# Gate and up projection of the second token half by seven block products, with the down projection summed in DRAM

## The chip, the cores and the metric

One core of a Trainium2 chip runs the whole program. The metric is the device time of one execution in microseconds (us). The engines are PE (matrix multiply; PEld is its weight load), ACT and DVE (element-wise), POOL and SP (here they mostly issue transfers). SBUF is the on-chip memory and PSUM the small memory that PE writes and that ACT and DVE read. DRAM is reached by transfers ("DMAs") which 16 DMA engines carry out.

## The reference

The reference is one transformer-like block on 2048 tokens of 1024 features: a state-space branch, a convolution branch, a merge, and a gated feed-forward network ("FFN") with a final norm. What matters here is its last part.

```
def _swiglu(h, wg, wu, wd):
    return (jax.nn.silu(h @ wg) * (h @ wu)) @ wd
...
        x = x + g2 * _swiglu(_modulate(x, norm2_g[l], sh2, sc2), w_ffn_gate[l], w_ffn_up[l], w_ffn_down[l])
...
    return _rmsnorm(x, norm_f_g)
```

The hidden width FFN_HIDDEN is 2816, which is 22 column tiles of 128. `wg` and `wu` are 1024 by 2816 and `wd` is 2816 by 1024, all 32-bit floats.

## The kernel before, in words

Tokens are handled in two halves of 1024 (HALF). Features lie on the partitions and tokens along the free axis. The 32-bit product is made of three PE products: each operand is split into a rounded part "hi" and a remainder "lo", and `gemm` (L181) issues hi by hi, hi by lo and lo by hi for each 128 features, all into one PSUM sum. The names tell the parts: `h2h`/`h2l` are the two parts of the normalised input, `ah`/`al` those of the hidden activations, `hi`/`lo` those of a weight tile. `wload` loads 512 KB of weights into `raw`, ACT makes `hi` (L159) and DVE `lo` (L161); there are two buffers each of raw, hi and lo.

`ffn` goes through the 22 hidden tiles in chunks of 2, 4, 4, 4, 4 and 4. For each hidden tile it computes gate (48 matmuls of 512 tokens: 8 feature blocks, 3 products, 2 token blocks) and up (48 more); ACT applies silu to gate (L1168), DVE multiplies by up (L1175), and `split` makes ah (ACT, L193) and al (DVE, L194). After a chunk come its "downs": for each of 8 output tiles m, PE multiplies ah/al by the down weights and DVE adds the result, times the modulation, to an SBUF accumulator `acc[m]` (L1190), which had been loaded once with the residual from the DRAM array `d_x1`. In the last chunk the downs run for tokens 0 to 511 and then for 512 to 1023; ACT squares the second lot (L1193) and DVE sums the squares (L1195).

Work beside this runs as "background" generators (`bg`): at each k step of a matmul group `tick` gives them credit, and they emit some of their instructions there. `h2` normalises the input that way (L1141 to 1144), and `final` the finished first 512 tokens (transposes L1244, Square L1247, `newton` L140 to 146 for the reciprocal root, scaling L1249). `final_last` does the last 512 tokens by matmuls with a diagonal of gains (L1225, L1232, L1233). `gains` builds that diagonal ahead of the second half's FFN (transpose L1206).

PSUM has eight banks of 512 numbers per partition. `mm` hands out tiles of two banks (three of them), `ms` tiles of one bank (two). `t4` hands out one of four SBUF buffers of 128 by 1024 numbers. A buffer is given out again once its last reader is done. Within one engine instructions run in the order of its list, so what stands behind a waiting instruction waits too. A scheduler fixes these lists when the program is built; blocks marked `high_priority` are drawn ahead in them.

Of the kernel before, what the change touches and what calls it, by code (L numbers as in the profile page):

```python
# [1524 lines left out]
```

## Time and profile before

| | |
|---|---|
| median of 3 runs | 3040.83 us (3038.77 to 3044.93) |
| the profiled execution's own time | 3038.56 us |
| its span from first to last instruction | 3036.8 us |
| mean granted PE clock | 0.991 |
| PE busy | 2963.6 us, 98% of the span |
| DVE busy | 1990.7 us, 66% |
| ACT busy | 905.9 us, 30% |

All times of single instructions come from the profiled execution. PE's row of busy time is a union of overlapping matmuls; a granted clock of 1.00 is 2.4 GHz and 0.50 is 1.2 GHz. The FFN of the second half runs from about 2200 us to the end.

### The profile page before, as it was taken

What the parts mean: (1) busy time and instruction counts of PE and PEld (TensorE: products, weight loads), DVE (VectorE), ACT (ScalarE), POOL (GpSimd) and SP (SyncE); (2) the same over time, 40 slices, a digit from 0 to 9 for tenths busy, and PEclk for the clock granted to TensorE, in tenths of its full rate; (3) what the DMA queues carried; (4) which work ended last, traced back from release to release, by engine and by line L of the source; (5) the groups of instructions that cost most, each with busy time, mean ns of one, the idle gap of its engine ahead of it and who ended that gap; (6) DMA issues with size and microseconds to landing.
All of it is one profiled execution on the core that took longest, in us unless ns stands there. A gap on an engine that the chain in (4) does not pass through costs nothing.

```text
span 3036.8 us, 34166 instructions
## 1 busy us (share of the span) xinstructions
PE 2963.6 (98%) x13227; PEld 2403.5 (79%) x13227; DVE 1990.7 (66%) x2932; ACT 905.9 (30%) x1235; POOL 172.9 (6%) x313
## 2 busy tenths in 40 slices
PE   7999999999999999999999999999999999999999
PEld 3778787878878777778888888888887888888887
DVE  6489899997897576767787887756666232322225
ACT  4323344334443562233212112134233111111112
POOL 0111321100011000000000000000000000000000
PEclk8999999999999999999999999999999999999999
DMA  5344545534443468865222222223556111111112
GB/s 202 125 124 127 156 151 185 175 94 124 125 121 110 156 202 289 273 199 184 69 63 63 63 63 72 67 97 122 190 179 203 56 49 49 49 49 49 49 49 104
DMA packets 386754, 370.36 MB, mean 122 GB/s; under 512 B 31841, under 2 KB 334273, under 8 KB 386592
## 3 DMA queue, kind: packets, MB, share of 16 engines
q1 hardware_dynamic: 347168, 280.97, 29.8%
q0 software_dynamic: 25968, 82.46, 7.6%
q10 hardware_dynamic: 13456, 4.75, 0.7%
q8 instruction: 104, 1.70, 0.2%
q14 instruction: 58, 0.48, 0.0%
HBM read 280.42 MB, written 87.67 MB: 121 GB/s over the span
## 4 chain that ended last, share of the span: by engine, by line
issue 66%; PE 20%; DVE 5%; DMA 5%; POOL 2%; ACT 1%; ACTq 0%; POOLq 0%; DVEq 0%; SPq 0%
PE mm L181 17%; DVE acc L919 2%; DMA wm<-in_w_mod_dram 2%; PE ms L740 1%; DMA d_xt<-xts 1%; DVE lo L161 1%; DMA ma<-d_ma 1%; POOL d_x L1111 1%; PE ms L695 1%; DMA d_in<-st 0%; DMA Braw<-in_ssm_b_re_dram 0%; DMA dwr<-in_dw_kernel_dram 0%; PE ms L805 0%; PE ms L806 0%; DVE mr L345 0%
## 5 line engine op out<-in xcount | busy, mean ns | idle before, releaser
L159 ACT ACTIVATE hi<-raw 128x1024 fp32r<-128x1024 f32 (+1 forms) x280 | 293.1, 1047 | 1317.7 <-PE mm L181 1259.9
L919 DVE SCALAR_TENSOR_TENSOR acc<-cin,dwk,acc 128x1009 f32<-128x1009 f32 (+1 forms) x464 | 570.3, 1270 | 1.1 <-ACT acc L915 0.5
L181 PE MATMUL mm<-h2h,hi 128*128 128x512 f32 x1408 | 548.6, 390 | 0.0
L181 PE MATMUL mm<-h2l,hi 128*128 128x512 f32 x1408 | 547.9, 389 | 0.1
L181 PE MATMUL mm<-h2h,lo 128*128 128x512 f32 x1408 | 547.8, 389 | 0.0
L161 DVE TENSOR_TENSOR lo<-raw,hi 128x1024 fp32r<-128x1024 f32 (+1 forms) x280 | 337.0, 1204 | 267.2 <-ACT hi L159 266.1
L181 PE MATMUL mm<-hh,hi 128*128 128x512 f32 x1152 | 479.1, 416 | 0.5 <-ACT hh L445 0.5
L181 PE MATMUL mm<-hl,hi 128*128 128x512 f32 x1152 | 454.7, 395 | 0.0
L181 PE MATMUL mm<-hh,lo 128*128 128x512 f32 x1152 | 453.8, 394 | 0.0
L181 PEld LDWEIGHTS mm<-h2l,hi 128*128 128x128 f32 x1408 | 264.4, 188 | 55.6 <-DVE h2l L1144 0.7
L181 PEld LDWEIGHTS mm<-h2h,hi 128*128 128x128 f32 x1408 | 264.3, 188 | 55.5 <-issue 0.5
L181 PEld LDWEIGHTS mm<-h2h,lo 128*128 128x128 f32 x1408 | 264.3, 188 | 54.7 <-DVE lo L161 0.2
L181 PE MATMUL mm<-ah,hi 128*128 128x512 f32 x704 | 274.5, 391 | 0.0
L181 PE MATMUL mm<-al,hi 128*128 128x512 f32 x704 | 273.8, 390 | 0.0
L181 PE MATMUL mm<-ah,lo 128*128 128x512 f32 x704 | 273.5, 389 | 0.0
L181 PEld LDWEIGHTS mm<-hh,lo 128*128 128x128 f32 x1152 | 218.1, 189 | 47.0 <-issue 0.4
L181 PEld LDWEIGHTS mm<-hh,hi 128*128 128x128 f32 x1152 | 218.1, 189 | 46.6 <-issue 2.2
L181 PEld LDWEIGHTS mm<-hl,hi 128*128 128x128 f32 x1152 | 218.5, 190 | 44.5 <-issue 1.4
L1175 DVE TENSOR_TENSOR fg<-mm,fg 128x1024 f32<-128x1024 f32 (+1 forms) x48 | 54.5, 1134 | 271.9 <-PE mm L181 266.6
L1190 DVE SCALAR_TENSOR_TENSOR x<-mm,mod,x 128x1024 f32<-128x1024 f32 (+1 forms) x104 | 124.6, 1199 | 162.6 <-PE mm L181 162.3
L181 PEld LDWEIGHTS mm<-ah,hi 128*128 128x128 f32 x704 | 132.1, 188 | 31.1 <-ACT ah L193 4.0
L181 PEld LDWEIGHTS mm<-al,hi 128*128 128x128 f32 x704 | 132.2, 188 | 28.5 <-DVE al L194 1.2
(376 smaller groups left out, 3718.6 us busy)
## 6 DMA issues: line engine op xcount, KB each, us to landing
raw<-in_w_in_dram SPq DMA_DIRECT2D x72, 512.0 KB
wm<-in_w_mod_dram SPq DMA_DIRECT2D x48, 512.0 KB
raw<-in_w_ffn_gate_dram SPq DMA_DIRECT2D x48, 512.0 KB
raw<-in_w_ffn_up_dram SPq DMA_DIRECT2D x48, 512.0 KB
raw<-in_w_ffn_down_dram SPq DMA_DIRECT2D x44, 512.0 KB
d_g<-gsig POOLq DMA_DIRECT2D x32, 512.0 KB, 4.5
raw<-in_w_out_dram SPq DMA_DIRECT2D x32, 512.0 KB
d_vp<-vsig POOLq DMA_DIRECT2D x16, 512.0 KB, 3.7
```

What stands on the lines that cost most here:

```text
L159: nc.scalar.activation(hi, raw, AF.Copy)
L161: nc.vector.tensor_tensor(lo, raw, hi.bitcast(F32), op=OP.subtract)
L181: nc.tensor.matmul(ps[:, b * bw : (b + 1) * bw], wt[:, k, c0 : c0 + 128], mv[k][:, b * bw : (b + 1) * bw], start=(k == 0 and j == 0), stop ...
L695: nc.tensor.matmul(pz[:, d, :], BD[:, d, i, r, :], CR[d][r][:, i, d : d + 8].rearrange("p j c -> p (j c)"), start=(r == 0), stop=(r == 1))
L740: nc.tensor.matmul(ps.rearrange("p (i m) -> p m i", i=8), IN[:, d, i, :], rhs, start=True, stop=True)
L919: self.behind(nc.vector.scalar_tensor_tensor(t, x[:, i : i + W], K(i), t, op0=OP.mult, op1=OP.add), LAG)
L1111: nc.gpsimd.dma_start(self.d_x1[m, :, ts], xt)
L1175: nc.vector.tensor_tensor(g, pu[:, cs], g, op=OP.mult)
L1190: nc.vector.scalar_tensor_tensor(acc[m][:, cs], ps[:, cs], self.mod2[:, 24 + m : 25 + m], acc[m][:, cs], op0=OP.mult, op1=OP.add)
```

## The change

The change concerns the second token half only. For one hidden tile, gate and up together are a product of a 2 by 2 block matrix of weights (gate and up; features 0 to 511 and 512 to 1023: A11, A12, A21, A22) with a 2 by 2 block matrix of inputs (the same two feature blocks; tokens 0 to 511 and 512 to 1023: B11, B12, B21, B22). Before, that is eight block products of 12 matmuls each. After, it is seven, by sums of blocks: S1 = A21 + A22, S2 = S1 - A11, S3 = A11 - A21, S4 = A12 - S2 for the weights, and T1 = B12 - B11, T2 = B22 - T1, T3 = B22 - B12, T4 = B21 - T2 for the inputs. The T blocks are made once (`sums_first`, `sums_last`), in the background of the first chunk; the S blocks for each hidden tile (`group_weights`). One hidden tile is then a `group` of 84 matmuls in place of 96: A11 B11, S1 T1, S2 T2, A12 B21, S3 T3, S4 B22 and A22 T4. Partial sums stay in PSUM: b1 and b2 are the two banks of one `mm` tile, b3 is an `ms` tile. Some of them are copied to the SBUF tiles `fg` and `fu` on the way (`copy` on ACT) and added later (`add` on DVE).

The SBUF that held the accumulators now holds these operands. So the downs are no longer summed in SBUF: ACT scales each result into a `t4` tile `fd`, and POOL issues a DMA that adds it to `d_x1` in DRAM. All chunks have 2 hidden tiles (11 chunks; the first is computed as before, by eight products). For the last chunk the sums are loaded back and finished as before. `gains` moves from the start of the FFN to after it. Cut to its core:

```
+    def prod(self, ps, w, c0, x, start=True, stop=True, group=True):
+
+        nc = self.nc
+        (whi, wlo), (xhi, xlo) = w, x
+        n = len(xhi)
+        for k in range(n):
+            for j, (wt, mv) in enumerate(((whi, xhi), (whi, xlo), (wlo, xhi))):
+                nc.tensor.matmul(
+                    ps,
+                    wt[:, k, c0 : c0 + 128],
+                    mv[k],
+                    start=start and k == 0 and j == 0,
+                    stop=stop and k == n - 1 and j == 2,
+                    skip_group_check=not group,
+                )
+            self.tick()
+
...
+    def group_weights(self, vp, t):
+
+        nc = self.nc
+        TT = nc.vector.tensor_tensor
+        col = slice(t * 128, (t + 1) * 128)
+        gate, up = (self.A[n][0, :, col].rearrange("(k p) c -> p k c", p=128) for n in ("w_ffn_gate", "w_ffn_up"))
+        with self.tc.high_priority():
+            w4 = self.wp.tile([128, 8, 128], F32, tag="raw", name=self.nm("wu"))
+            nc.sync.dma_start(w4, up)
+            w1, w2, w3 = (vp.tile([128, HALF], F32, tag="acc", name=self.nm("ws"), bufs=3).rearrange("p (k c) -> p k c", c=128) for _ in range(3))
+            a, b = slice(0, 4), slice(4, 8)
+            nc.sync.dma_start(w1[:, a], gate[:, a])
+            nc.sync.dma_start(w2[:, b], gate[:, b])
+            TT(w1[:, b], w4[:, a], w4[:, b], op=OP.add)
+            TT(w2[:, a], w1[:, b], w1[:, a], op=OP.subtract)
+            p1 = self.parts(w1)
+            TT(w3[:, a], w1[:, a], w4[:, a], op=OP.subtract)
+            TT(w3[:, b], w2[:, b], w2[:, a], op=OP.subtract)
+            p2 = self.parts(w2)
+            p3 = self.parts(w3)
+            p4 = self.parts(w4[:, b], 512)
+        cut = lambda p, s: tuple(t[:, s] for t in p)
+        return {"A11": cut(p1, a), "S1": cut(p1, b), "S2": cut(p2, a), "A12": cut(p2, b), "S3": cut(p3, a), "S4": cut(p3, b), "A22": p4}
+
+    def group(self, vp, t, X, ah, al):
+
+        nc = self.nc
+        W = self.group_weights(vp, t)
+        ps, b3 = self.mm(), self.ms()
+        b1, b2 = ps[:, 0:512], ps[:, 512:1024]
+        g, u = self.t4(name="fg"), self.t4(name="fu")
+        L, R = slice(0, 512), slice(512, 1024)
+        copy = lambda o, i: nc.scalar.activation(o, i, AF.Copy)
+        add = lambda o, i: nc.vector.tensor_tensor(o, i, o, op=OP.add)
+        hp = self.tc.high_priority
+        self.prod(b1, W["A11"], 0, X["B11"], group=False)
+        with hp():
+            copy(g[:, L], b1)
+        self.prod(b2, W["S1"], 0, X["T1"], group=False)
+        with hp():
+            copy(u[:, R], b2)
+        self.prod(b1, W["S2"], 0, X["T2"], start=False, group=False)
+        with hp():
+            copy(g[:, R], b1)
+        self.prod(b3, W["A12"], 0, X["B21"])
+        with hp():
+            add(g[:, L], b3)
+            nc.scalar.activation(g[:, L], g[:, L], AF.Silu)
+        self.prod(b1, W["S3"], 0, X["T3"], start=False, group=False)
+        with hp():
+            add(u[:, R], b1)
+        self.prod(b2, W["S4"], 0, X["B22"], start=False, group=False)
+        with hp():
+            add(g[:, R], b2)
+            nc.scalar.activation(g[:, R], g[:, R], AF.Silu)
+            nc.vector.tensor_tensor(u[:, R], u[:, R], g[:, R], op=OP.mult)
+        self.prod(b1, W["A22"], 0, X["T4"], start=False, group=False)
+        with hp():
+            nc.vector.tensor_tensor(u[:, L], b1, g[:, L], op=OP.mult)
+            self.split(u, ah, al)
+        self.dve(12)
...
+        for c in range(11):
+            if c:
+                for t in range(2):
+                    self.group(vp, c * 2 + t, X, *a[t])
+                    yield "up"
+            if c == 10:
+                break
+            for m4 in range(2):
+                w = down(c, m4)
+                for m in range(4):
+                    ps = self.mm()
+                    for b in range(2):
+                        self.prod(ps[:, b * 512 : (b + 1) * 512], w, m * 128, halves[b])
+                    o = self.t4(name="fd")
+                    nc.scalar.activation(o, ps, AF.Copy, scale=self.mod2[:, 24 + m4 * 4 + m : 25 + m4 * 4 + m])
+                    nc.gpsimd.dma_start(self.d_x1[m4 * 4 + m, :, hs], o, accum_op=OP.add)
+                    yield "down"
+        acc = [self.slot("Q", F32, name="x1") for _ in range(8)]
+        rs.append(self.slot("P", F32, (128, 512), name="rsf"))
+        with self.tc.high_priority():
+            for m in range(8):
+                nc.gpsimd.dma_start(acc[m], self.d_x1[m, :, hs])
+        end.append(acc)
+        for b in range(2):
+            bs = slice(b * 512, (b + 1) * 512)
+            for m in range(8):
+                if m % 4 == 0:
+                    w = down(10, m // 4)
+                ps = self.mm()[:, bs]
+                self.prod(ps, w, (m % 4) * 128, halves[b])
+                nc.vector.scalar_tensor_tensor(acc[m][:, bs], ps, self.mod2[:, 24 + m : 25 + m], acc[m][:, bs], op0=OP.mult, op1=OP.add)
+                if b:
+                    sq = rs[0] if m == 0 else self.t4(shape=(128, 512), name="sq")
+                    nc.scalar.activation(sq, acc[m][:, bs], AF.Square)
+                    if m:
+                        nc.vector.tensor_tensor(rs[0], rs[0], sq, op=OP.add)
+                self.dve()
+                yield "down"
...
+        X, rs, end = {}, [], []
+        e = self.bg(self.h2s_first(1, r[2], X))
         take(self.out_proj(1, mg[1], vp, 512, 512, r))
         self.finish(e)
-        acc = []
-        dg = self.gains(vp)
-        rs = [vp.tile([128, HALF], F32, tag="acc", name="rsf", bufs=3)[:, 0:512]]
-        f1 = self.ffn(1, h2[1], "P", acc, 1, rs)
-        e = self.bg(self.h2(1, r[3], "Q", h2, 512, 512))
+        X["raw"] = [self.slot("P", F32, name="bf") for _ in range(4)]
+        for n in ("T2", "T3"):
+            X[n] = self.operand("P", n)
...
+        def sums():
+            yield from self.sums_first(X)
+            yield (W_SUM,)
+            yield from self.sums_last(X)
+
+        e = self.bg(sums())
+        take(f1, 2 + 8)
+        self.finish(e)
+        take(f1, 10 * 2 + 9 * 8 + 8)
+        acc = end[0]
+        dg = self.gains()
         e = self.bg(self.final(1, acc, 0, 4))
         take(f1)
         self.finish(e)
```

The lists of the engines show where the new instructions stand. The first place is ACT while gate and up are computed. Before, its list for a hidden tile and the start of the next reads as follows: `fg` from `mm` is the silu of gate, `ah` the first part of the activations, `hi` that of the next weights.

```order
L1168 ACTIVATE fg_19053<-mm_19004 128x1024 [waits PE_49]
L159 ACTIVATE hi_19174<-raw_19172 128x1024 [waits DMAHW2_49,DVE_49,PE_49]
L193 ACTIVATE ah_19110<-fg_19053 128x1024 [waits DVE_49]
L159 ACTIVATE hi_19234<-raw_19232 128x1024 [waits DMAHW3_49,PE_49,Activation_49]
L1168 ACTIVATE fg_19170<-mm_19121 128x1024 [waits PE_49]
```

After, one group on ACT. `fg` and `fu` from `mm` are the copies of partial sums (L1346), L1361 and L1368 the two silus, L1309 the first parts of S and A weights (`ws`, `wu`), and the last line the split.

```order
L1346 ACTIVATE fg_18356<-mm_18354 128x512 [waits DMASW2_49,PE_49,Activation_49]
L1309 ACTIVATE hi_18346<-ws_18331 128x1024 [waits DVE_49,PE_49]
L1346 ACTIVATE fu_18357<-mm_18354 128x512 [waits DMASW3_49,PE_49,Activation_49]
L1309 ACTIVATE hi_18350<-wu_18327 128x512 [waits DMAHW2_49,DVE_49,PE_49]
L1346 ACTIVATE fg_18356<-mm_18354 128x512 [waits PE_49]
L1361 ACTIVATE fg_18356<-fg_18356 128x512 [waits DVE_49]
L1309 ACTIVATE hi_18463<-ws_18456 128x1024 [waits DMAHW0_49,PE_49,Activation_49]
L1368 ACTIVATE fg_18356<-fg_18356 128x512 [waits DVE_49]
L1309 ACTIVATE hi_18469<-ws_18457 128x1024 [waits DMAHW1_49,PE_49,Activation_49]
L194 ACTIVATE ah_16974<-fu_18357 128x1024 [waits DVE_49]
```

Before, ACT reads PSUM once for each hidden tile (L1168). Now it reads it three times (L1346), a weight part stands between each two of these reads, and that part itself waits for PE, since it goes into a buffer from which PE has to be done.

The second place is PE. Before, its list at the step from gate to up of a hidden tile reads:

```order
L181 MATMUL mm_19644<-h2l_16657,hi_19640 128x512
L181 MATMUL mm_19644<-h2h_16649,lo_19642 128x512
L181 MATMUL mm_19704<-h2h_16642,hi_19700 128x512 [waits Activation_49]
L181 MATMUL mm_19704<-h2l_16650,hi_19700 128x512
L181 MATMUL mm_19704<-h2h_16642,lo_19702 128x512 [waits DVE_49]
```

In that list one product ends, and the next begins in another PSUM tile. After, a group's list from the end of S2 T2 over one matmul of A12 B21 (`ms`) to the start of S3 T3 reads:

```order
L1295 MATMUL mm_18354<-T2h_16967,lo_18344 128x512
L1295 MATMUL ms_18355<-B21h_16651,lo_18344 128x512
L1295 MATMUL mm_18354<-T3h_16970,hi_18346 128x512 [waits Activation_49]
L1295 MATMUL mm_18354<-T3l_16972,hi_18346 128x512
L1295 MATMUL mm_18354<-T3h_16970,lo_18348 128x512 [waits DVE_49]
```

S3 T3 goes into the PSUM tile of S2 T2. The step from S3 T3 to S4 B22, a few matmuls on, reads:

```order
L1295 MATMUL mm_18354<-T3h_16971,hi_18346 128x512
L1295 MATMUL mm_18354<-T3l_16973,hi_18346 128x512
L1295 MATMUL mm_18354<-T3h_16971,lo_18348 128x512
L1295 MATMUL mm_18354<-B22h_16654,hi_18346 128x512 [waits DVE_49]
L1295 MATMUL mm_18354<-B22l_16656,hi_18346 128x512
```

Before, the new gate or up product goes to another PSUM tile (`mm_19704` in place of `mm_19644`), and the waits are for weights. After, all products but A12 B21 go to the same tile `mm_18354`. The wait of S3 T3 is for the copy of `fg` out of that tile (the fifth ACT line above), the wait of S4 B22 for DVE's add of `fu` out of it, and S1 T1, S2 T2 and A22 T4 begin with a wait of the same kind. A group's 12 matmuls of A12 B21 stand in three lots: 4 between A11 B11 and S1 T1, 7 between S1 T1 and S2 T2, and 1 as shown.

On DVE the same group ends with this run: the `add` of `fg` from b3, the second part of A22's weights, the `add` of `fu` from b1, the `add` of `fg` from b2, work for the next group, and the two products.

```order
L1347 TENSOR_TENSOR fg_18356<-ms_18355,fg_18356 128x512 [waits DMASW6_49,DMASW2_49,PE_49]
L1311 TENSOR_TENSOR lo_18352<-wu_18327,hi_18350 128x512 [waits Activation_49]
L1347 TENSOR_TENSOR fu_18357<-mm_18354,fu_18357 128x512 [waits DMASW7_49,DMASW3_49,PE_49]
L1347 TENSOR_TENSOR fg_18356<-mm_18354,fg_18356 128x512 [waits PE_49,Activation_49]
L1311 TENSOR_TENSOR lo_18465<-ws_18456,hi_18463 128x1024 [waits Activation_49]
L1369 TENSOR_TENSOR fu_18357<-fu_18357,fg_18356 128x512 [waits Activation_49]
L1327 TENSOR_TENSOR ws_18723<-wu_18721 128x512 [waits DMAHW2_49,DVE_49]
L1372 TENSOR_TENSOR fu_18357<-mm_18354,fg_18356 128x512 [waits PE_49]
```

Before, DVE read PSUM once for each hidden tile here (L1175); now it does so four times (L1347 three times, L1372).

The third place is PE at the end of the program. Before, the transposes of `final` (`ident`) stand between the last downs:

```order
L181 MATMUL mm_21115<-ah_20744,hi_21094 128x512
L181 MATMUL mm_21115<-al_20745,hi_21094 128x512
L181 MATMUL mm_21115<-ah_20744,lo_21096 128x512
L1244 MATMUL mm_21132<-ident,x_2392_16976 128x128 [waits DVE_49,PE_49]
L1244 MATMUL mm_21132<-ident,x_2393_16977 128x128
```

So the list has 128x128 transposes among 128x512 matmuls. After, the last down and the first transposes read:

```order
L1295 MATMUL mm_21532<-ah_16976,hi_21495 128x512
L1295 MATMUL mm_21532<-al_16977,hi_21495 128x512
L1295 MATMUL mm_21532<-ah_16976,lo_21497 128x512
L1493 MATMUL mm_21545<-ident,x_3010_21339 128x128 [waits DMASW6_49,DVE_49]
L1493 MATMUL mm_21545<-ident,x_3011_21340 128x128 [waits DMASW7_49]
```

Three sets of eight transposes follow one another; behind the third the list goes on with the sums over the squares (`rsf`) and the products with the gains (`gfd`):

```order
L1493 MATMUL mm_21603<-ident,x_3016_21345 128x128
L1493 MATMUL mm_21603<-ident,x_3017_21346 128x128
L962 MATMUL ms_21661<-onesm,rsf_21347 128x1 [waits DVE_49]
L962 MATMUL ms_21661<-onesm,rsf_21347 128x1 x3
L1474 MATMUL ms_21726<-gfd_21436,x_3010_21339 128x128 [waits PE_49]
```

No transpose stands between downs any more.

## Rows read from the trace of the kernel before

**Rows 1.** part 1 (busy us, share, instructions) and the granted clock of part 2

```profile
PE 2963.6 (98%) x13227; PEld 2403.5 (79%) x13227; DVE 1990.7 (66%) x2932; ACT 905.9 (30%) x1235; POOL 172.9 (6%) x313
...
PEclk8999999999999999999999999999999999999999
```

**Rows 2.** busy us of PE, PEld, DVE, ACT, POOL; then PEclk, DMA share, GB/s

```profile
2400.00:2500.00 100.00, 100.00 (x442) 82.50 (x441) 27.98 (x23) 14.56 (x14) 0.00 (x0) 1.00 0.17 51
```

**Rows 3.** timeline: start us, length us, engine, line, operation, [idle before <- releaser]

```profile
2450.67 0.39 PE L181 MATMUL mm<-h2l,hi 128*128 128x512 f32 x1
...
2450.89 0.39 PE L181 MATMUL mm<-h2h,lo 128*128 128x512 f32 x1
...
2451.09 1.06 ACT L159 ACTIVATE hi<-raw 128x1024 fp32r<-128x1024 f32 x1 [8.86 <-PE mm L181]
...
2451.39 1.23 DVE L1175 TENSOR_TENSOR fg<-mm,fg 128x1024 f32<-128x1024 f32 x1 [8.81 <-PE mm L181]
...
2452.65 1.06 ACT L193 ACTIVATE ah<-fg 128x1024 fp32r<-128x1024 f32 x1 [0.49 <-DVE fg L1175]
...
2582.24 1.23 DVE L1175 TENSOR_TENSOR fg<-mm,fg 128x1024 f32<-128x1024 f32 x1 [8.81 <-PE mm L181]
```

**Rows 4.** instruction groups, 2200 to 3037 us: count | busy us, mean ns | idle before

```profile
L161 DVE TENSOR_TENSOR lo<-raw,hi 128x1024 fp32r<-128x1024 f32 x87 | 106.1, 1220 | 174.5 <-ACT hi L159 174.0
L159 ACT ACTIVATE hi<-raw 128x1024 fp32r<-128x1024 f32 x87 | 92.2, 1060 | 579.1 <-PE mm L181 574.2 <-issue 3.8 <-ACT h2h L1142 0.6
...
L194 DVE TENSOR_TENSOR al<-fg,ah 128x1024 fp32r<-128x1024 f32 x20 | 24.5, 1225 | 0.0
...
L193 ACT ACTIVATE ah<-fg 128x1024 fp32r<-128x1024 f32 x20 | 21.2, 1060 | 9.9 <-DVE fg L1175 9.9
...
L1249 DVE SCALAR_TENSOR_TENSOR o<-mm,ny,gf 128x1024 f32<-128x1024 f32 x4 | 5.1, 1281 | 0.0
...
L1175 DVE TENSOR_TENSOR fg<-mm,fg 128x512 f32<-128x512 f32 x4 | 2.7, 686 | 4.3 <-PE mm L181 4.3
L161 DVE TENSOR_TENSOR lo<-raw,hi 128x512 fp32r<-128x512 f32 x4 | 2.7, 684 | 3.2 <-ACT hi L159 3.2
...
L159 ACT ACTIVATE hi<-raw 128x512 fp32r<-128x512 f32 x4 | 2.5, 632 | 17.0 <-PE mm L181 17.0
```

**Rows 5.** timeline, two places where PE waits for an element-wise result

```profile
1285.17 1.22 DVE L194 TENSOR_TENSOR mgl<-gb,mgh 128x1024 fp32r<-128x1024 f32 x1
...
1286.44 0.79 PE L181 MATMUL mm<-mgl,hi 128*128 128x512 f32 x1 [0.84 <-DVE mgl L194]
...
1358.52 0.75 DVE L1110 SCALAR_TENSOR_TENSOR xt<-mm,mod,xt 128x512 f32<-128x512 f32 x1 [1.46 <-DMA xt<-d_xt]
...
1359.41 0.47 PE L181 MATMUL mm<-mgh,hi 128*128 128x512 f32 x1 [1.78 <-DVE xt L1110]
...
1359.72 0.40 PE L181 MATMUL mm<-mgl,hi 128*128 128x512 f32 x1
```

**Rows 6.** the same columns, three stretches outside the second FFN

```profile
1145.00:1150.00 5.00, 4.71 (x14) 3.43 (x13) 2.85 (x3) 1.94 (x2) 0.00 (x0) 0.66 0.78 270
1285.00:1290.00 5.00, 4.06 (x9) 2.54 (x10) 3.95 (x6) 2.06 (x3) 0.00 (x0) 0.66 0.59 159
1355.00:1360.00 5.00, 3.22 (x15) 2.39 (x14) 2.68 (x5) 1.47 (x3) 0.44 (x1) 1.00 0.65 174
```

**Rows 7.** page, parts 3 (packets, MB, share of 16 engines) and 6 (KB, us to landing)

```profile
q1 hardware_dynamic: 347168, 280.97, 29.8%
q0 software_dynamic: 25968, 82.46, 7.6%
...
d_g<-gsig POOLq DMA_DIRECT2D x32, 512.0 KB, 4.5
```

**Rows 8.** what PE waited for, 2190 to 3037 us: total, times, longest

```profile
PE ms L1206 <- DMA gfr<-in_norm_f_g_dram: 1.0, 1, 1.0
```

**Rows 9.** timeline, the last matmul of the down projection

```profile
3020.82 0.39 PE L181 MATMUL mm<-ah,lo 128*128 128x512 f32 x1
```

More of the change, by code (lines that the diff above doesn't have):

```diff
@@ L1198, in ffn, with operand, h2s_first @@
             c0 += cn
-    def gains(self, vp):
+    def operand(self, S, name):
+        parts = [[self.slot(S, name=name + p) for _ in range(2)] for p in "hl"]
+        return [[t[:, c : c + 512] for t in p for c in (0, 512)] for p in parts]
+    def h2s_first(self, hf, rs, X):
+        nc = self.nc
+        ts = slice(hf * HALF, hf * HALF + 512)
+        yield (4,)
+        rstd = self.rstd_small(rs, 4)
+        yield 1.5
+        yield (4,)
+        row = yield from self.rstd_row(rstd, 4)
+        for n in ("B11", "T1", "B21", "B22"):
+            X[n] = self.operand("Q", n)
+        for k in range(8):
+            x = self.t4(name="x1t")[:, 0:512]
+            nc.sync.dma_start(x, self.d_x1[k, :, ts])
+            hi, lo = X["B11" if k < 4 else "B21"]
+            h, l = hi[k % 4], lo[k % 4]
+            s, b = self.s2[:, k : k + 1], self.mod2[:, 8 + k : 9 + k]
+            nc.vector.tensor_tensor(x, x, row[:, 0:512], op=OP.mult)
+            nc.scalar.activation(x, x, AF.Identity, scale=s, bias=b)
+            nc.scalar.activation(h, x, AF.Copy)
+            nc.vector.tensor_tensor(l, x, h.bitcast(F32), op=OP.subtract)
+            yield 1.5
@@ new lines, in h2s_second @@
+    def h2s_second(self, hf, rs, X, vp):
+        nc = self.nc
+        ts = slice(hf * HALF + 512, (hf + 1) * HALF)
+        yield (4,)
+        rstd = self.rstd_small(rs, 4)
+        yield 1.5
+        yield (4,)
+        row = yield from self.rstd_row(rstd, 4)
+        t = [vp.tile([128, HALF], F32R, tag="acc", name=self.nm("b12"), bufs=3) for _ in range(3)]
+        t.append(vp.tile([128, HALF + 30], F32R, tag="cin", name="b12_l", bufs=2))
+        X["B12"] = [[t[p][:, c : c + 512] for p in q for c in (0, 512)] for q in ((0, 1), (2, 3))]
+        for k in range(4):
+            f = X["raw"][k]
+            for g in range(2):
+                nc.sync.dma_start(f[:, g * 512 : (g + 1) * 512], self.d_x1[k + 4 * g, :, ts])
+            for g in range(2):
+                x = f[:, g * 512 : (g + 1) * 512]
+                kk = k + 4 * g
+                s, b = self.s2[:, kk : kk + 1], self.mod2[:, 8 + kk : 9 + kk]
+                h, l = (p[k] for p in X["B22" if g else "B12"])
+                nc.vector.tensor_tensor(x, x, row[:, 0:512], op=OP.mult)
+                nc.scalar.activation(x, x, AF.Identity, scale=s, bias=b)
+                nc.scalar.activation(h, x, AF.Copy)
+                nc.vector.tensor_tensor(l, x, h.bitcast(F32), op=OP.subtract)
+            yield 2.8
@@ new lines, in sums_first @@
+    def sums_first(self, X):
+        nc = self.nc
+        TT = nc.vector.tensor_tensor
+        for k in range(4):
+            f = X["raw"][k]
+            b12, b22 = f[:, 0:512], f[:, 512:1024]
+            u, v = self.t4(name="tu"), self.t4(name="tv")
+            g, t1, t2, t3 = u[:, 0:512], u[:, 512:1024], v[:, 0:512], v[:, 512:1024]
+            TT(g, X["B11"][0][k].bitcast(F32), X["B11"][1][k].bitcast(F32), op=OP.add)
+            TT(t1, b12, g, op=OP.subtract)
+            TT(t3, b22, b12, op=OP.subtract)
+            TT(t2, b22, t1, op=OP.subtract)
+            for n, t in (("T1", t1), ("T2", t2), ("T3", t3)):
+                self.split(t, X[n][0][k], X[n][1][k])
+                yield 1.4
@@ new lines, in sums_last @@
+    def sums_last(self, X):
+        nc = self.nc
+        TT = nc.vector.tensor_tensor
+        X["T4"] = self.operand("P", "T4")
+        for k in range(4):
+            u = self.t4(name="tw")
+            g, t2 = u[:, 0:512], u[:, 512:1024]
+            TT(g, X["B21"][0][k].bitcast(F32), X["B21"][1][k].bitcast(F32), op=OP.add)
+            TT(t2, X["T2"][0][k].bitcast(F32), X["T2"][1][k].bitcast(F32), op=OP.add)
+            TT(g, g, t2, op=OP.subtract)
+            self.split(g, X["T4"][0][k], X["T4"][1][k])
+            yield 2.8
@@ new lines, in parts @@
+    def parts(self, f, c=1024):
+        nc = self.nc
+        hi = self.wp.tile([128, c // 128, 128], F32R, tag="hi", name=self.nm("hi"))
+        nc.scalar.activation(hi, f, AF.Copy)
+        lo = self.wp.tile([128, c // 128, 128], F32R, tag="lo", name=self.nm("lo"))
+        nc.vector.tensor_tensor(lo, f, hi.bitcast(F32), op=OP.subtract)
+        return hi, lo
+    def group_weights(self, vp, t):
+        nc = self.nc
+        TT = nc.vector.tensor_tensor
+        col = slice(t * 128, (t + 1) * 128)
[17 more added lines that the diff above has]
+        return {"A11": cut(p1, a), "S1": cut(p1, b), "S2": cut(p2, a), "A12": cut(p2, b), "S3": cut(p3, a), "S4": cut(p3, b), "A22": p4}
@@ L1206, in gains @@
         nc.tensor.transpose(ps, row, self.ident[0:8, 0:8])
-        dg = vp.tile([128, HALF], F32, tag="acc", name="gfd", bufs=3)
+        dg = self.slot("P", F32, name="gfd")
         for k in range(8):
```

40 lines of the change are left out of this document (38 added, 2 removed).

## The prediction

> **What bounds the kernel now.** I read the page first, then the stretch that the change touches. PE is busy 98% of the span at a clock near full [rows 1]. Between 2400 and 2500 us it is busy 100.00 of 100 us, at granted clock 1.00, while DVE works 28 us and ACT 15 [rows 2]. There is no wait of PE in this stage, so its time is the number of matmuls times their pace. For the pace I take the same instruction of two chunks: the DVE multiply at 2451.39 and at 2582.24 us [rows 3]. Between them lie 576 matmuls (4 hidden tiles of 96, 8 downs of 24), so one costs 130.85 / 576 = 0.2272 us. A matmul taken away here is worth that, and any wait put in front of PE is lost in full, because nothing else is late.
>
> **What goes: matmuls.** The groups cover 20 hidden tiles (the first chunk keeps eight products), each 12 matmuls shorter: 240 x 0.2272 = -54.5 us, or 2.73 per group.
>
> **What comes: waits inside a group.** Before, each product had a PSUM tile of its own. Now six of seven share one tile, and the lists show each of the five steps between them waiting for the read of the product just ended. By the data only S3's wait is needed; the others are for a read of the other bank. The lists alone don't say when these reads are done; the trace does:
> - After the start of a product's last matmul, ACT begins 0.42 us later (2450.67 to 2451.09; the buffer it waited for was freed by the last matmul but one) and DVE 0.50 us later (2450.89 to 2451.39) [rows 3].
> - One read of 128x512 takes 0.686 us on DVE; on ACT I take 0.63, and a 128x1024 weight part 1.06 [rows 4].
> - PE follows 0.05 to 0.14 us after: DVE's mgl runs from 1285.17 to 1286.39 and PE starts at 1286.44; xt runs from 1358.52 to 1359.27, PE starts at 1359.41. The next matmul then starts 0.31 later, not 0.23: about 0.1 more [rows 5].
>
> With s the start of a product's last matmul:
> - S1 after A11: four matmuls of A12 lie between, S1 is due at s+1.14, the copy ends at s+1.05. Nothing.
> - S2 after S1: on ACT a weight part of 1.06 us stands ahead of the copy and itself waits for S1's eleventh matmul (s+0.19 to 1.25), then the copy to 1.8. Seven matmuls of A12 lie between; S2 is due at s+1.82. About 0.05.
> - S3 after S2: again a weight part ahead (s+0.19 to 0.82), copy to 1.4, PE at 1.43. One matmul lies between, so S3 is due at 0.45: 0.98 + 0.1 = 1.08.
> - S4 after S3: DVE's add runs from s+0.50 to 1.19, PE starts at about 1.28, due at 0.23: 1.05 + 0.1 = 1.15.
> - A22 after S4: the same, 1.15.
>
> The sum is 3.43 us per group (2.95 with the short handoffs and no slow restart, 3.7 with the long ones), against 2.73 saved: 20 x 3.43 = +68.6 us (59 to 74). The row nearest to this case, 1.22 us of DVE work behind which PE stood idle 0.84 [rows 5], lies between; I keep 3.43.
>
> **Group to downs.** After the second group of each chunk the downs need its activations at once: DVE's last multiply s+0.50 to 1.19, ah on ACT 1.22 to 2.28, al on DVE behind a weight part, 2.41 to 3.64 [rows 4]. Twelve matmuls need none of it, al is due at s+2.95: 0.84 us with handoff and restart, x10 = +8.4 (5 to 12). Before, the newest hidden tile stood last of four in the downs, and nothing waited there [rows 2].
>
> **First chunk.** Beside its 288 matmuls (65.4 us) DVE now makes the T blocks, the second input half and the first group's weights: some 60 operations of 0.685 us and 15 of 1.22 [rows 4], 59 us. That is a queue nearly full, with buffers waited for in turn: 0 to 12 us, taken as +5, since 59 is below 65.
>
> **Accumulating DMAs.** No row of before shows one. There are 80 of 512 KB, one per down (2.73 us each), on POOL's queue, which is otherwise idle there. The copies of a group need their t4 buffers: m4's DMA must be done at its first copy, m5's at its second. With T the start of the downs, the first is issued at about T+4.7 and the copy is due at T+24.9, so five of them may take 20 us: up to 4 us each costs nothing. The lower bound is a plain transfer on this queue: 82.46 MB at 7.6% of 16 engines over 3036.8 us is 22 GB/s per engine, so 1.5 us. The upper one is the time to land, 4.5 us, as if they didn't overlap [rows 7]: 2.3 us per chunk, +21. I take +3, nearer to the lower end, whose row is a throughput.
> The Trainium skill, in "DMA: Bandwidth & Descriptors" (section "Rules for kernel authors"), says an accumulating DMA reads its destination and writes it later. If so, each moves 512 KB twice; no run here shows it. By the queue's row that is 3 us, still under 4, and the sum stays; it is why I give the slow case more than a token chance.
>
> **The end.** Before, the program ends 16.0 us after the last down's last matmul [rows 9], since most of `final` lies between the downs. Now four sets of transposes, four reciprocal roots and four scalings of 1.28 us [rows 4] all stand behind it: three more scalings (3.8 us) and roots on DVE, less the transposes that no longer lengthen the downs. +4 (2 to 8). The loads of the eight sums hide behind the last two groups (over 40 us).
>
> **Gains moved.** PE's wait of 1.0 us for them goes [rows 8]: -1.
>
> **Sum.** -54.5 + 68.6 + 8.4 + 5 + 3 + 4 - 1 = +33.5. The profiled execution took 3038.56 us, 2.3 below the median of 3040.83; so 3072 beside it, and **3074 us** beside the median.
>
> **Rivals.**
> 1. *Waits that don't bind: faster.* If a group's waits cost under 1.75 us, the change pays: -54.5 + 8.4 + 5 + 3 + 4 - 1 = -35, and 35 / 20 = 1.75. The mechanism would be that the reads end before PE reaches the step, as for S1, at S4 and A22 too; with S3's wait alone (1.1 us, 22 in all) the time is 3041 - 13 = 3028. For it: ACT and DVE are mostly idle [rows 2]. Against it: 0.50 + 0.69 us of a free DVE is already five matmuls, and only one slot is between. 6%.
> 2. *Accumulating DMAs bind.* From 4 us each on, the group's copies wait for buffers: at 5 us T+4.7+25 against T+24.9, 4.8 us per chunk, x9 = 43, so 3114; at 5.5 us some 3140. Against it: DMA engines are 17% busy here [rows 2]. 12%.
> 3. *The clock falls.* PE went to 1.2 GHz where it had stood still repeatedly: 0.66 in 1285 to 1290, with 9 matmuls started where a full stretch has 22; after one stall of 1.78 us at 1359 it stayed at 1.00 [rows 5, 6]. At 0.66 those 5 us give up 1.7 us. Three stalls per group stand 3.9 us apart; one such drop in each group would be 20 x 1.7 = +34, 3108. The Trainium skill, in "TensorE: Matmul & The Clock Gate" (section "A second HAM failure mode: psum-queue depth-cycling"), tells of just this: PE "micro-idles between MM groups frequently enough that HAM oscillates" when it cycles through PSUM banks. [...] 6%.
> 4. *About even.* Waits of 1.6 to 1.9 us per group give 3035 to 3047. It needs shorter handoffs than any row has. 5%.
>
> **Chances.** The forecast has 71%, the rivals 6, 12, 6 and 5. Its own range is 3056 to 3095, from the bounds of the waits, first chunk and end. The range to hold 8 in 10 runs from **3048 to 3116**: it takes in most of rivals 2 and 3 and leaves out 1 and 4. About 0.2% (6 us) is what a measurement of this kernel can tell from no change: faster 7%, within 5%, slower 88%.
>
> **What would show it.** PE's busy share falls to some 95%, with matmul count 240 lower, yet the span is longer. The list of waits has PE <- ACT fg L1346 about 20 times near 1.0 us, PE <- DVE fu L1347 and fg L1347 about 20 times each near 1.0, and PE <- DVE al L195 about 10 times near 0.8. A group lasts 22.4 us, a chunk 67.5 rather than 65.4. Wrong, if a group lasts under 20.8 us (rival 1), if PE or ACT waits for the DMAs on `d_x1` (2), or if the clock's row shows sixes and sevens after 2270 us (3).

## The result: slower by 1.2%, as forecast, with one term mis-sized

The changed kernel took 3075.93 us in the median (3071.25 to 3084.87, 4 runs) beside 3042.23 for the kernel before: ratio 1.0115, interval 1.0088 to 1.0142. Run again later beside ten runs of before (3045.16), it took 3083.42, ratio 1.0122 (1.0107 to 1.0136). The forecast was 3074.

The profiled execution took 3084.87 us (span 3083.1), at the long end of its runs, while the profile of before lies at the short end of its own. So the two profiles differ by 46 us where the medians differ by 34 and 38. Of the 46, 4.3 arise ahead of the second FFN, where both kernels do the same work (1.6 in a second profile of the changed kernel); the FFN itself grew from 742.7 to 784.7 us (785.6 in the second profile). The accounts below are of the FFN.

The page of the changed kernel, parts 1 and 2 (busy us, share, instructions; granted clock in 40 slices), answers to [rows 1]: 240 matmuls fewer, and PE busy 96% where it was 98.

```profile
PE 2945.7 (96%) x12987; PEld 2357.3 (76%) x12987; DVE 2089.6 (68%) x3116; ACT 1075.6 (35%) x1463; POOL 245.3 (8%) x401
...
PEclk9999999999999999999999999999999999999999
```

The view by stretch (us, then busy us and instructions of PE, PEld, DVE, ACT, POOL; clock, DMA share, GB/s) answers to [rows 2]. Before, PE was busy all of 100 us with 442 matmuls. Now it starts 386 in 100 us at the same clock; the second row is one whole chunk of 264 matmuls, 67.91 us where I had 67.5.

```profile
2450.00:2550.00 100.00, 91.58 (x386) 70.73 (x386) 40.97 (x50) 36.63 (x45) 6.85 (x8) 1.00 0.43 97
2582.18:2650.09 67.91, 62.63 (x266) 48.62 (x264) 25.27 (x30) 25.83 (x31) 6.82 (x8) 1.00 0.50 110
```

What PE waited for from 2190 us on (us in all, times, longest) shows the four waits that the prediction named, as many times as it named them, though each is shorter in this list (0.5 to 0.9 us in the mean) than the 0.8 and 1.0 that it gave. The fifth row is one it did not place.

```profile
PE mm L1295 <- DVE fg L1347: 17.5, 20, 1.2
PE mm L1295 <- DVE fu L1347: 15.7, 20, 0.8
PE mm L1295 <- ACT fg L1346: 15.0, 21, 0.8
PE mm L1295 <- DVE al L195: 4.9, 10, 0.5
PE mm L1295 <- ACT fd L1424: 3.2, 2, 2.7
```

The timeline (start us, length us, then the instruction and what it waited for) of the middle of a group shows how two of them come about.

```profile
2592.84 0.39 PE L1295 MATMUL mm<-T2h,lo 128*128 128x512 f32 x1
...
2593.04 0.63 ACT L1309 ACTIVATE hi<-wu 128x512 fp32r<-128x512 f32 x1 [2.86 <-PE mm L1295]
2593.07 0.39 PE L1295 MATMUL ms<-B21h,lo 128*128 128x512 f32 x1
...
2593.58 0.58 ACT L1346 ACTIVATE fg<-mm 128x512 f32<-128x512 f32 x1
...
2594.21 0.50 PE L1295 MATMUL mm<-T3h,hi 128*128 128x512 f32 x1 [0.75 <-ACT fg L1346]
...
2596.84 0.39 PE L1295 MATMUL mm<-T3h,lo 128*128 128x512 f32 x1
2597.26 0.69 DVE L1347 TENSOR_TENSOR fu<-mm,fu 128x512 f32<-128x512 f32 x1 [2.48 <-PE mm L1295]
...
2598.01 0.50 PE L1295 MATMUL mm<-B22h,hi 128*128 128x512 f32 x1 [0.78 <-DVE fu L1347]
```

S2's last matmul starts at 2592.84. ACT takes the weight part `hi` first (2593.04) and the copy of `fg` after it (2593.58); PE starts S3 at 2594.21, one matmul of A12 having filled 0.23 us of 1.37. In the same way S3's last matmul starts at 2596.84, DVE's add runs from 2597.26, and S4 starts at 2598.01 with nothing in between. Before, the same handoff delayed nobody [rows 3], since the next product had its own tile. PE's idle time in the brackets understates each stop: the matmul before it runs out over 0.16 us, and the first one after it takes 0.34 to the next (0.31 in [rows 5]).

The step from the second group of a chunk to its downs:

```profile
2627.16 0.39 PE L1295 MATMUL mm<-T4h,lo 128*128 128x512 f32 x1
...
2627.58 0.69 DVE L1372 TENSOR_TENSOR fu<-mm,fg 128x512 f32<-128x512 f32 x1 [1.13 <-PE mm L1295]
...
2628.37 1.04 ACT L194 ACTIVATE ah<-fu 128x1024 fp32r<-128x1024 f32 x1
2628.50 1.23 DVE L1391 TENSOR_TENSOR lo<-wd,hi 128x1024 fp32r<-128x1024 f32 x1 [0.23 <-ACT hi L1389]
...
2629.64 1.22 DVE L195 TENSOR_TENSOR al<-fu,ah 128x1024 fp32r<-128x1024 f32 x1
...
2630.92 0.50 PE L1295 MATMUL mm<-al,hi 128*128 128x512 f32 x1 [0.49 <-DVE al L195]
```

The group's last matmul starts at 2627.16. DVE multiplies, ACT makes `ah`, DVE does a weight part (`lo`) and then `al`, and PE stands still until 2630.92; its thirteenth matmul of the downs was due at 2630.1.

### The profile page after: what moved, and what is told of

The parts are those of the page before. It is cut to its first block, busy times and chain, and to the rows that moved or that the text cites. A ratio compares the mean times of both kernels' runs of the same rounds, so it can differ in the third digit from the quotient of the medians.

```text
span 3083.1 us, 34510 instructions
## 1 busy us (share of the span) xinstructions
PE 2945.7 (96%) x12987; PEld 2357.3 (76%) x12987; DVE 2089.6 (68%) x3116; ACT 1075.6 (35%) x1463; POOL 245.3 (8%) x401
## 4 chain that ended last, share of the span: by engine, by line
issue 51%; PE 32%; DVE 7%; DMA 5%; POOL 2%; ACT 2%; ACTq 0%; POOLq 0%; DVEq 0%; SPq 0%
PE mm L182 16%; PE mm L1295 11%; DVE acc L920 2%; DMA wm<-in_w_mod_dram 1%; PE ms L1295 1%; PE ms L741 1%; POOL d_x L1425 1%; DMA d_xt<-xts 1%; DVE lo L162 1%; DMA d_x<-fd 1%; PE ms L696 1%; POOL d_x L1112 1%; DMA Braw<-in_ssm_b_im_dram 0%; DMA dwr<-in_dw_kernel_dram 0%; PE mm L312 0%
## 5 line engine op out<-in xcount | busy, mean ns | idle before, releaser
L160 ACT ACTIVATE hi<-raw 128x1024 fp32r<-128x1024 f32 (+1 forms) x212 | 222.7, 1050 | 770.1 <-PE mm L182 726.5
L162 DVE TENSOR_TENSOR lo<-raw,hi 128x1024 fp32r<-128x1024 f32 (+1 forms) x212 | 256.5, 1210 | 93.4 <-ACT hi L160 93.0
L182 PE MATMUL mm<-h2h,hi 128*128 128x512 f32 x704 | 274.8, 391 | 0.0
L182 PE MATMUL mm<-h2l,hi 128*128 128x512 f32 x704 | 273.9, 389 | 0.1
L182 PE MATMUL mm<-h2h,lo 128*128 128x512 f32 x704 | 273.9, 389 | 0.0
L182 PEld LDWEIGHTS mm<-hh,hi 128*128 128x128 f32 x1152 | 218.4, 190 | 46.6 <-issue 2.2
L1311 DVE TENSOR_TENSOR lo<-ws,hi 128x1024 fp32r<-128x1024 f32 x60 | 73.5, 1225 | 230.6 <-ACT hi L1309 229.6
L182 PEld LDWEIGHTS mm<-h2l,hi 128*128 128x128 f32 x704 | 132.2, 188 | 27.9 <-DVE h2l L1145 0.5
L182 PEld LDWEIGHTS mm<-h2h,hi 128*128 128x128 f32 x704 | 132.2, 188 | 27.6 <-issue 0.3
L182 PEld LDWEIGHTS mm<-h2h,lo 128*128 128x128 f32 x704 | 132.2, 188 | 27.5
```

The costliest lines, as they stand in the source:

```text
L160: nc.scalar.activation(hi, raw, AF.Copy)
L162: nc.vector.tensor_tensor(lo, raw, hi.bitcast(F32), op=OP.subtract)
L182: nc.tensor.matmul(ps[:, b * bw : (b + 1) * bw], wt[:, k, c0 : c0 + 128], mv[k][:, b * bw : (b + 1) * bw], start=(k == 0 and j == 0), stop ...
L1311: nc.vector.tensor_tensor(lo, f, hi.bitcast(F32), op=OP.subtract)
```

## The experiments

**A PSUM tile for each of b1 and b2.** This undoes what the waits inside a group are put down to; the engines' lists then follow from it.

```
-        ps, b3 = self.mm(), self.ms()
-        b1, b2 = ps[:, 0:512], ps[:, 512:1024]
+        b1, b2, b3 = self.mm()[:, 0:512], self.mm()[:, 0:512], self.ms()
```

> Theory: the loss is PE's waits inside a group, and these come from b1 and b2 being halves of one PSUM tile. With a tile each, S2 no longer waits for the read of S1, S4 not for the add after S3, and A22 not for the add after S4; twelve matmuls of A12 lie between S2 and S3 in PE's list. The 3.35 us of waits per group should go nearly whole: 20 x 3.35 = 67 us, so about 3009 (3002 to 3018), a group of 19.1 to 19.4 us, and the list of waits without ACT fg, DVE fu and DVE fg. Rival: the reads of PSUM themselves are the limit (seven of them per group beside 15 weight operations), so the waits move to the next group's start: 3045 to 3070, a group of 21 us or more. What the data need (S3's wait alone) would leave 1 us per group: about 3030.

Measured: 3011.09 us (3007.0 to 3014.65), ratio to before 0.9886 (0.9864 to 0.9908). The rival of reads as the limit is out: nothing moved to the next group. All twelve matmuls of A12 now run between S2 and S3, so the one wait that the data need, S3's for the copy of `fg`, has twelve matmuls before it in place of one. Of PE's waits from 2330 us on, al and the second chunk's start are left, and in the groups one of 0.5 us (last row); the rows left out are single waits in the first chunk and at the end:

```profile
PE mm L1295 <- DVE al L195: 4.5, 10, 0.5
PE mm L1295 <- ACT fd L1423: 3.4, 2, 2.9
...
PE mm L1295 <- ACT fg L1345: 0.5, 1, 0.5
```

Two groups, by stretch, in the changed kernel and then with two tiles: 168 matmuls in 45.21 us, 40.43 of them busy, against 38.08 of 38.08.

```profile
2446.36:2491.57 45.21, 40.43 (x169) 30.76 (x168) 20.21 (x25) 15.04 (x20) 0.85 (x1) 1.00 0.35 82
```

```profile
2502.45:2540.53 38.08, 38.08 (x170) 31.53 (x168) 19.99 (x25) 15.34 (x20) 0.85 (x1) 1.00 0.40 95
```

So a group's waits cost (45.21 - 38.08) / 2 = 3.56 us, 71 us in all; the prediction had 3.43 and 69.

**The second token block first.** In addition, tokens 512 to 1023 are split before the last product, and the downs take them first.

```
+            self.split(u[:, R], ah[:, R], al[:, R])
...
-            self.split(u, ah, al)
+            self.split(u[:, L], ah[:, L], al[:, L])
...
-                    for b in range(2):
+                    for b in (1, 0):
```

> As the kernel with two tiles, and the activations of tokens 512 to 1023, which are ready a product earlier, are split at once, with the downs taking these tokens first. Theory: the 1.33 us of wait at the step from a chunk's second group to its downs (al) goes in each of 10 chunks: 12 us less than with two tiles alone, about 2997 (2990 to 3006). Rival: the longer list on ACT and DVE (four half splits for two whole ones) delays other steps and nothing is gained: 3005 to 3015.

Measured: 3015.62 us (3009.65 to 3019.58), 0.9904 (0.9882 to 0.9926): no gain, as the rival said (its range ended at 3015); the downs take 22.77 to 22.81 us, against 22.71 to 22.75 with two tiles alone. Its timeline at that step tells why, and it is not the longer list that the rival named.

```profile
2535.60 0.39 PE L1295 MATMUL mm<-T4h,lo 128*128 128x512 f32 x1
...
2535.85 1.06 ACT L1389 ACTIVATE hi<-wd 128x1024 fp32r<-128x1024 f32 x1 [1.14 <-issue]
2536.03 0.69 DVE L1372 TENSOR_TENSOR fu<-mm,fg 128x512 f32<-128x512 f32 x1
...
2536.82 1.13 ACT L194 ACTIVATE ah<-fu 128x512 fp32r<-128x512 f32 x2
2536.95 1.23 DVE L1391 TENSOR_TENSOR lo<-wd,hi 128x1024 fp32r<-128x1024 f32 x1 [0.23 <-ACT hi L1389]
...
2538.09 1.29 DVE L195 TENSOR_TENSOR al<-fu,ah 128x512 fp32r<-128x512 f32 x2
...
2539.43 0.50 PE L1295 MATMUL mm<-al,hi 128*128 128x512 f32 x1 [0.53 <-DVE al L195]
```

Both halves of `ah` stand behind the weight part of 1.06 us on ACT (x2 at 2536.82), and both halves of `al` behind the one of 1.23 on DVE. The data were ready earlier; the place in the lists was not. PE still waits, to 2539.43.

**The older hidden tile first.** With two PSUM tiles again, the first three downs of a chunk do their 18 matmuls on the older hidden tile before those on the newest.

```
+                pend = []
                 for m in range(4):
...
+                    if not pend:
+                        pend = [self.mm() for _ in range(3 if m == 0 and m4 == 0 else 1)]
+                        for k in range(2):
+                            wk = tuple(x[:, k : k + 1] for x in w)
+                            for i, ps in enumerate(pend):
+                                for b in range(2):
+                                    xk = [x[k : k + 1] for x in halves[b]]
+                                    self.prod(ps[:, b * 512 : (b + 1) * 512], wk, (m + i) * 128, xk, start=k == 0, stop=k == 1, group=False)
+                    ps = pend.pop(0)
...
```

> As the kernel with two tiles, and in the first three downs of a chunk the 18 matmuls on the older hidden tile come first, those on the newest after them (before: 9 and then the newest). Theory: al of the newest tile is ready about 3.7 us after the start of the group's last matmul and was due at 2.5 to 3; after 18 matmuls it is due at 4.3 to 4.7, so the wait of 1.33 us goes in each of 10 chunks: about 2998 (2991 to 3005), against 3011 for two tiles alone, with no PE wait for al but in the last chunk. Rival: as with the tokens split, al comes later by as much as it is due later, since weight parts stand ahead of it on ACT and DVE, and the time stays at 3008 to 3016.

Measured: 3001.87 us (3000.03 to 3003.53), 0.9868 (0.9851 to 0.9884), 9 less than two tiles alone. One whole chunk by stretch, to be held against the 67.91 us above:

```profile
2712.25:2772.09 59.84, 59.84 (x265) 49.55 (x264) 25.02 (x31) 26.15 (x30) 6.84 (x8) 1.00 0.56 123
```

PE is busy all of it; 59.84 us is 264 times 0.2267. I had expected 13 us, having counted the stop as 1.33 from its bracket and neighbours. By the length of the downs (22.75 us with two tiles, 21.76 here) it was 0.99.

**Plain writes in place of adding ones.**

```
-                    nc.gpsimd.dma_start(self.d_x1[m4 * 4 + m, :, hs], o, accum_op=OP.add)
+                    nc.gpsimd.dma_start(self.d_x1[m4 * 4 + m, :, hs], o)
```

> The changed kernel with its 80 DMAs to DRAM writing in place of adding, so the sum over the chunks is left out. Theory: the accumulation costs next to nothing in time, since only one group start waited for one (0.7 us) beside a late start after the first chunk: within 5 us of the changed kernel, 3070 to 3077, though the DMAs land in 3 to 5 us in place of 8.2. Rival: accumulating DMAs are behind the changed kernel's loss and its spread between runs: 3040 to 3065, and a smaller spread.

Measured: 3072.96 us (3064.79 to 3077.39), 1.0091 (1.0066 to 1.0115). The time agrees with the theory, but the margin hid something: in its profile the second chunk begins without the wait `PE <- ACT fd`. The spread of the runs, 12.6 us, hardly shrank either (13.6 for the changed kernel). The queue and the DMA from issue to landing (packets, MB, share of 16 engines; KB each, us), from 2330 us on, of the changed kernel and of this one:

```profile
q0 software_dynamic: 13248, 48.24, 33.0%
...
d_x<-fd POOLq DMA_DIRECT2D x80, 512.0 KB, 8.2
```

```profile
q0 software_dynamic: 13248, 48.24, 16.1%
...
d_x<-fd POOLq DMA_DIRECT2D x80, 512.0 KB, 2.9
```

**Plain writes in the first chunk only**, to find where that matters.

```
-                    nc.gpsimd.dma_start(self.d_x1[m4 * 4 + m, :, hs], o, accum_op=OP.add)
+                    nc.gpsimd.dma_start(self.d_x1[m4 * 4 + m, :, hs], o, **({"accum_op": OP.add} if c else {}))
```

> The changed kernel with only the first chunk's eight DMAs writing in place of adding (their sum with the residual is left out). Theory: in the first chunk the adding DMAs land late (8.2 us) while the T4 sums take two of the four t4 buffers, so evictions and with them the second chunk's start wait; the later 72 DMAs are hidden. In the profile the first chunk and the first group should take 9 us less than in the changed kernel's profile (4 to 12), and the time 5 to 9 us less than the changed kernel run again beside it: 3067 to 3071. Rival: the first chunk is slow because DVE's queue is full, whatever the DMAs do: no difference (within 2 us).

Beside it the changed kernel once more:

> The changed kernel itself once more, so that the one with the first chunk's plain writes has its time beside it, and its first profile (3084.87 us, the longest of its four runs) a second one. Theory: 3076 (3072 to 3080), the same waits in the groups (17.5, 15.7 and 15.0 us in all); the wait of 2.7 us at the second chunk's start and the fall of the clock after it come again, since they follow from the order. Rival: they were an accident of that run, and a usual run has a first chunk and first group 5 us or more shorter.

Measured: 3077.16 us (3066.05 to 3083.57), 1.0102 (1.0082 to 1.0121), against 3083.42 (3078.61 to 3084.13) for the changed kernel: 6 less, though the intervals overlap. The profiles are plainer. From the FFN's start to the downs of the second chunk they take 114.8 us here, 125.3 and 127.4 in the two profiles of the changed kernel. The timeline of the first profile of the changed kernel there (ACT, one row of DVE, PE):

```profile
2360.72 1.11 ACT L1424 ACTIVATE fd<-mm,mod 128x1024 f32<-128x1024 f32 x1 [3.26 <-DMA d_x<-fd]
...
2365.05 0.69 DVE L1282 TENSOR_TENSOR tw<-B21h,B21l 128x512 f32<-128x512 f32 x1 [1.01 <-DMA d_x<-fd]
...
2371.89 1.11 ACT L1424 ACTIVATE fd<-mm,mod 128x1024 f32<-128x1024 f32 x1 [2.42 <-DMA d_x<-fd]
...
2373.06 0.50 PE L1295 MATMUL mm<-B11h,hi 128*128 128x512 f32 x1 [2.69 <-ACT fd L1424]
```

The evictions `fd` wait 3.26 and 2.42 us for DMAs that have not landed. The sums of the T blocks take t4 buffers in turn with them in this chunk: `tu` and `tv` of T1 to T3 are read until 2358.35, and two `tw` of T4 begin at 2365.05 and 2367.51, each after a DMA's landing as well. So an eviction waits for the DMA issued two evictions earlier, and the PSUM tile that the second chunk wants comes free 2.69 us late. With plain writes:

```profile
2359.28 1.12 ACT L1424 ACTIVATE fd<-mm,mod 128x1024 f32<-128x1024 f32 x1 [0.79 <-DMA d_x<-fd]
...
2367.23 1.12 ACT L1424 ACTIVATE fd<-mm,mod 128x1024 f32<-128x1024 f32 x1 [0.96 <-DMA d_x<-fd]
...
2370.20 0.39 PE L1295 MATMUL mm<-ah,lo 128*128 128x512 f32 x1
2370.43 0.39 PE L1295 MATMUL mm<-B11h,hi 128*128 128x512 f32 x1
```

The same waits are 0.79 and 0.96, and the second chunk follows at once. DVE has the same work in both, so its full queue, the rival, is not what cost these 10 us. In the second profile of the changed kernel the wait at its start was 3.9 us, so it is no accident of one run; the groups' waits came again as 17.4, 15.7 and 13.8 us. Its time lies above the 3072 to 3080 expected, in runs where before took 3 us more as well. In the first profile of the changed kernel the second chunk's first matmuls then run at a lower clock (view by stretch, clock third from the end):

```profile
2375.00:2380.00 5.00, 3.38 (x9) 1.82 (x7) 3.10 (x5) 3.55 (x5) 1.70 (x2) 0.74 0.93 179
2380.00:2385.00 5.00, 4.38 (x12) 3.46 (x13) 3.07 (x5) 0.63 (x1) 0.00 (x0) 0.66 0.93 168
```

Both are means of the two levels, 1.2 and 2.4 GHz. At 0.74 and 0.66 these 10 us give up some 3 us.

**Eight products in the new frame.** The groups are replaced by eight block products, and the T and S sums left out.

```
-                    self.group(vp, c * 2 + t, X, *a[t])
...
+                    wg = self.wload(A["w_ffn_gate"][0, :, col])
+                    pg = self.mm()
+                    for b in range(2):
+                        self.prod(pg[:, b * 512 : (b + 1) * 512], wg, 0, xs[b])
...
-        e = self.bg(sums())
```

> The changed kernel with eight block products as before and no T or S sums: only the small chunks, the sum in DRAM and the new end are left of the change. Theory: these cost a chunk's wait for al (1.3 us x 10), 8 us at the end, and little else: about 3064 (3056 to 3072). Together with 54 us for the 240 matmuls and 67 of waits in the groups this adds up to the changed kernel's 3076. Rival: the sum in DRAM binds (3085 or more), or all of the loss is in the groups (3042).

Measured: 3063.33 us (3054.29 to 3065.53), 1.0055 (1.0037 to 1.0073). As expected: what the seven products come with (small chunks, the sum in DRAM, the end) costs about 20 us by itself, before any group has waited. This kernel also settles the first chunk. Its DMAs add to DRAM and land as late as the changed kernel's (8.6 us), but no T sums take t4 buffers: no eviction waits for a DMA, the first chunk takes 70.2 us, and the second follows at once. So the loss there takes both, DMAs that land late and T sums.

**The end between the last downs.** To the kernel with the older tile first:

```
+        self.rate = 4.0
         e = self.bg(self.final(1, acc, 0, 4))
```

> As the kernel with 18 matmuls first, and the credit per tick is raised to 4 for the last downs, so that the transposes, roots and scalings of the final norm of tokens 512 columns earlier stand between the last downs again. Theory: the 8 us that the new end costs is mostly this order: 3 to 6 us less, about 2994 (2988 to 3001). Rival: the end is bound by DVE (a sum, a square's add and a scaling for each down) whatever the order: within 2 us of the kernel without it.

Measured: 2996.91 us (2994.66 to 3000.93), 0.9851 (0.9837 to 0.9866), 5 less in the medians, though the intervals overlap, and 2.6 in the profiles, of which 1.8 arise ahead of the FFN. From the start of the last down's last matmul to the end it takes 16.5 us in place of 23.9, but the last downs grow, since PE now waits there for DVE:

```profile
PE mm L1295 <- DVE nv L141: 1.3, 1, 1.3
PE mm L1295 <- DVE nt L146: 1.2, 1, 1.2
PE mm L1295 <- DVE x L1446: 0.8, 1, 0.8
```

From the last chunk's first down to the end the two profiles take 46.6 and 46.0 us. So by the profiles DVE takes back nearly all of the 7.4, as the rival said; where the 5 us of the medians arise isn't known. This is the best version run, 1.5% faster than before.

## Why the prediction was right, and where it was not

All in us, for the FFN in the two profiled executions (before 742.7, after 784.7, so +42.0):

| term | predicted | measured | from |
|---|---|---|---|
| 240 matmuls | -54.5 | -54.4 | 240 x 0.2267, the pace of the full chunk above |
| waits in 20 groups | +68.6 | +71.3 | 45.21 against 38.08 per two groups |
| al, 10 chunks | +8.4 | +9.5 to 9.9 | downs of 22.71 and 22.75 against 21.76 |
| first chunk, gains, adding DMAs | +7 | +11.3 | first chunk 74.7 against 70.0, the second chunk's two groups 5.4 longer than later ones, two groups of a later chunk 1.2 longer (46.43 against 45.2) |
| end | +4 | +4.2 | below |
| sum | +33.5 | +42 | |

- *The waits in a group* came step by step as worked out: S1 and S2 about 0.1 each, S3 1.02 (1.08 predicted), S4 1.05 and A22 1.12 (1.15 each). DVE answered after 0.42 us at S4 and 0.49 at A22, for 0.50. A slightly slower pace after each stop (0.23 to the next for several matmuls) and the 0.1 at S1 give back what these were smaller. One slip cost nothing: the working names 0.63 us for ACT's copy but ends the copies at 1.8 and 1.4, which is a copy of 0.58, and 0.58 is what it takes (2593.58 above). That it was the shared tile, and that the reads are no limit in themselves, is shown by the kernel with two tiles. Rivals 1 and 4 needed shorter handoffs than any row had, and the 0.42 was not short enough.
- *al* was underrated by 0.1 to 0.15 per chunk. Its fix was not obvious: taking the ready tokens first failed on the lists' order, taking the older tile first removed it.
- *The adding DMAs* are the step that failed. The prediction asked only when the later groups' copies need a t4 buffer, and found them safe up to about 4 us each. In that place it was nearly right, but with little to spare. The DMAs took 8.2 us each and overlapped, so that one landed every 2.5 to 3.0 us. In a usual chunk the fifth, issued at 2575.68, landed after 8.3 us, 1.2 before the copy that needs its buffer (2585.15). In one chunk of ten a copy waited 1.7 us for it, and PE 0.8. The landing time of 8.2 us lies beyond the 4.5 that I had taken from [rows 7] as the upper end.
- *The first chunk* is where it failed. What the prediction did not ask is who else takes these four buffers: here the T sums do, so evictions come to wait for DMAs issued shortly before them. The 10.5 and 12.6 us that the plain writes save there, against the two profiles of the changed kernel, are all of that place's loss (4.7 and 5.4 in the first profile, some 3 of it by the lower clock), for which I had taken +5 on account of DVE's queue. With plain writes the first chunk takes 69.0 us, no more than before's 70.0. The rival of binding DMAs was right in kind at this one place, and the sign named for it, ACT waiting for a DMA on `d_x1`, did show. The Trainium skill's rule in "DMA: Bandwidth & Descriptors" (section "Rules for kernel authors"), an accumulating DMA reads its destination and writes it later, fits a queue share that doubles, 33.0% against 16.1.
- *The end*: 24.4 us pass from the start of the last down's last matmul to the end, against 16.0. Of these 8.4 us go off 4.2 by which the downs of before had been longer than at the pace of 0.2267: 2.7 in the last chunk, where the transposes stood (46.55 us against 43.81 in the others), and 0.3 in each of the five full chunks (43.81 against 43.52), where PE waited a little for the newest `ah`. That second part the prediction had at nothing.
- *Gains* did not move behind the FFN but into a stop in the last group: its transpose runs at 3024.67 while S3 waits. The last two groups take 45.2 us like the others, so it costs nothing, as predicted.
- *The clock* (rival 3) fell in the chunks only at the start of the second one, after the stop of 2.69 us that ended at 2373.06, and stayed at 1.00 through all later groups with their three stops of about 1 us each. The stop alone does not tell when it falls: with two tiles PE stood still for 2.89 us at the same place (to 2379.16), and the clock of that kernel stayed at 1.00:

```profile
2380.00:2385.00 5.00, 4.89 (x22) 3.72 (x20) 3.21 (x6) 3.80 (x5) 1.09 (x2) 1.00 0.90 145
```

The first rows of the end, to be held against [rows 9]: 24 transposes come in a row behind the last down, and the last of the four scalings of tokens 0 to 511 starts 13.5 us later.

```profile
3058.95 2.79 PE L1493 MATMUL mm<-ident,x 128*128 128x128 f32 x24
...
3072.47 1.28 DVE L1498 SCALAR_TENSOR_TENSOR o<-mm,ny,gf 128x1024 f32<-128x1024 f32 x1
```

By the profiles the change costs 42 us in the FFN, by the medians 34 and 38 in all. Where the runs without a profile are shorter isn't known, so that the total came within 2 us is in part luck; that it lies 30 to 40 us above before isn't.

## What to carry to other kernels

Where PE is the bound, as here, an algorithm with fewer products paid only once each product's PSUM read had another product to hide behind: count the tiles that the waits are kept for, not the banks that the data need, and put an independent product between a sum's last matmul and its next use. When a buffer's user changes from an engine to a DMA, list everyone who takes a buffer from that pool while the DMA is in flight, in the start-up stage too. An operation made ready earlier gained nothing where it stood behind another in its engine's list.
